# A value and gate projection over paired high and low weights, with output-weight remainders on GpSimd

## The chip, the cores and the metric

The kernel runs on one core of one Trainium2 chip. The metric is the device time of one execution in microseconds (us), as the median of several runs. Lower is better. The core's engines appear under the profile's names: PE (matrix products; PEld is its weight load), DVE (vector work), ACT (activation functions and copies), POOL (GpSimd) and SP (which issues most loads).

## The reference

The program is one step of a two-layer model on 128 context tokens and 512 latent tokens, 640 in all, of width 1024. Layer 0 is gated attention. Layer 1, the one that the change touches, is a bidirectional gated linear recurrence with eight heads of 128 channels. Cut to what matters:

```python
proj = h @ w_in                      # 640 x 1024 times 1024 x 5120
q, f_fw, f_bw, i_in, g = split(proj) # five parts of 1024, 128 columns per head
qh, vh = silu(q), i_in               # vh: the values
forget = lb + (1 - lb) * sigmoid(f)  # for each direction
...                                  # scan over the tokens, forward and backward
o = rms_norm(o_fw + flip(o_bw))
out = (o * silu(g)) @ w_out          # g: the output gate
```

Products are in float32. The kernel carries an operand as a high part in a reduced format (`F32R`) and a low part, the remainder, and adds three products: high by high, high by low, low by high.

## The kernel before, in words

All activations of the 640 tokens stay on the chip: `h1hi` and `h1lo` are the two parts of layer 1's input, with the 1024 channels in eight blocks k of 128 and the tokens along the free axis. They are cut into five tiles tt of 128 tokens.

**A head's projection** is `proj_gen`. `load_vg` brings the weights of the head's values and output gate (1024 channels by 128 + 128 columns) as two pieces of 128 x 1024, each a raw load by SP, a high part by ACT (`L242`) and a low part by DVE (`L243`); both are done by `split_piece`. `vg_mms(tt)` (from L1331) makes the 256 columns of one token tile from 8 x 3 matmuls of 256 columns (L1338 to L1340), in PSUM tiles `vgps` of which the first holds four token tiles and the second one. `evac_vg` (from L1354) copies the values out by ACT, takes the gate's sigmoid by ACT, and multiplies it with the gate by DVE (L1364). Then follow three projections of 48 matmuls of 320 columns (`rps`, L1348 to L1350): queries, and the two forget gates.

**A head's recurrence** is `gla_gen`. It has seven levels (`lv`, L1481 for the first five), in which keys and queries in the big tile `A` are scaled in place by DVE between the levels: L1490 scales the keys ("A kv" in what follows), ACT copies them (`kc`, L1459), L1494 joins the decays (`nxt`, in tiles `T` and `Tb`), and L1495 scales the queries ("A q"). Level 1 needs A kv, the keys' copy and A q of level 0. After the levels come `dg`, the transposes `kp`, the state sums `sp`, the output `op` (L1544 to L1547), its normalisation `on` (L1555, L1558), the transposes `oT` (L1563) and the parts `ghi` (ACT) and `glo` (DVE, L1566) of the head's result. POOL computes `rstdo`, copies the near blocks to `At` (L1509), and works on residual rows of layer 0 (L1593 to L1595).

**The order.** The recurrence of head h runs beside the projection of head h+1. `Lane` merges them: `proj_gen` yields a number after each group of matmuls, the lane adds them to a virtual clock, and `gla_gen` continues when the clock passes what it last yielded (`D_LEV` = 2.3 between levels, `D_OUT` = 5.5 between `op` and `oT`). That sets the program order on every engine; each engine then runs its queue in order and waits at semaphores. The last head's recurrence has no projection beside it: there `tail_steps` puts in output products (`outp`, L1185 to L1187) of the finished heads, and splits the last five of eight pieces of the output weights, each by `wo_piece`: ACT makes the high part, DVE the low (L243). The first three pieces are split in `wo_early`, during the last head's projection.

Of the kernel before, what the change touches and what calls it, by code (L numbers as in the profile page):

```python
# [23 lines left out]
NT = TT * P  # L24
CW = 256
# [110 lines left out]
def hybrid_step(ctx: ExitStack, tc: tile.TileContext, a: dict, o: dict):  # L136
    nc = tc.nc
# [11 lines left out]
    def bank2(name):  # L149
        return pools["b2"].tile([P, 2, 512], F32, tag="b2", name=name)  # L150
# [1019 lines left out]
    h1lo = h1p.tile([P, KT, NT], F32R, tag="h1lo", name="h1lo")  # L1170
    wr = rpool("wr", 2)
# [128 lines left out]
    def wide(ps):  # L1300
        return ps[:].rearrange("p a b -> p (a b)")

    def proj_gen(h, H, first):
        loc, wvg = {}, []

        def tiles():
            H["A"] = g2.tile([P, 4 * NT], F32, tag="A", name="A")
            H["T"] = g2.tile([P, 2 * NT], F32, tag="T", name="T")
            for n in ("v", "g"):
                H[n] = g2.tile([P, NT], F32, tag=n, name=n)  # L1310
            loc["q"] = g1.tile([P, NT], F32, tag="q", name="q")

        def load(i, spare=None):
            if spare is None:
                hi = wr.tile([P, 1024], F32R, tag="whi", name="rhi")[:]
                lo = wr.tile([P, 1024], F32R, tag="wlo", name="rlo")[:]
            else:
                w = spare.tile([P, 2, 1024], F32R, tag="gate" if spare is gsp else "A", name="wspare")
                hi, lo = w[:, 0, :], w[:, 1, :]
            split_piece(hi, lo, ("rec_w_in", h, i), nc.vector)  # L1320
            return hi, lo

        def load_q(i, spare=None):
            w = load(i + 2, spare)
            loc[i] = [bank2("rps")] + [t.rearrange("p (k n) -> p k n", k=KT) for t in w]

        def load_vg(spare):
            for i in range(2):
                wvg.append([t.rearrange("p (k n) -> p k n", k=4) for t in load(i, spare if i else None)])

        def vg_mms(tt):  # L1331
            if tt % 4 == 0:
                loc["vg", tt // 4] = bank2("vgps")
            out = wide(loc["vg", tt // 4])[:, tt % 4 * CW:(tt % 4 + 1) * CW]
            t = slice(tt * P, (tt + 1) * P)
            for k in range(KT):
                hi, lo = (w[:, k % 4, :] for w in wvg[k // 4])
                nc.tensor.matmul(out, h1hi[:, k, t], hi, start=(k == 0), stop=False)  # L1338
                nc.tensor.matmul(out, h1hi[:, k, t], lo, start=False, stop=False)  # L1339
                nc.tensor.matmul(out, h1lo[:, k, t], hi, start=False, stop=(k == KT - 1))  # L1340
                if k % 4 == 3:
                    yield 1.28

        def mms(i, j):
            ps, hi, lo = loc[i]
# [5 lines left out]
                if k % 4 == 3:  # L1351
                    yield 1.6

        def evac_vg():  # L1354
            s = g1.tile([P, NT], F32, tag="s", name="s")
            for i, n in ((0, 4), (1, 1)):
                pv = wide(loc["vg", i])[:, :n * CW].rearrange("p (t e d) -> p e t d", t=n, e=2)
                c = slice(i * 4 * P, (i * 4 + n) * P)

                def tok(t):  # L1360
                    return t[:, c].rearrange("p (t d) -> p t d", t=n)
                nc.scalar.copy(tok(H["v"]), pv[:, 0])
                nc.scalar.activation(tok(s), pv[:, 1], AF.Sigmoid)
                nc.vector.tensor_tensor(tok(H["g"]), pv[:, 1], tok(s), ALU.mult)  # L1364

        def evac(i):
            pv = loc[i][0][:, :, :320]
# [23 lines left out]
            load_q(0)  # L1391
        for tt in range(TS):
            yield from vg_mms(tt)
        if first:
            load_q(0, g2)
        yield from vg_mms(TS)
# [15 lines left out]
    H = {}  # L1412
# [33 lines left out]
    nc.scalar.dma_start(mst, a["masks"])  # L1446
    nc.vector.tensor_copy(masks, mst)
    def gla_gen(h, H):
        A, T, v, g = H["A"], H["T"], H["v"], H["g"]
# [74 lines left out]
        yield D_KT  # L1524
        sp = bank2("sp")
        for i, c in enumerate((0, 1, 2, 4, 1, 2, 3, 4)):
            nc.tensor.matmul(wide(sp)[:, i * P:(i + 1) * P], kt[:, i * P:(i + 1) * P], v[:, c * P:(c + 1) * P], start=True, stop=True)
# [13 lines left out]
        opw = wide(op)  # L1541
        for c in range(TT):
            cc = slice(c * P, (c + 1) * P)
            nc.tensor.matmul(opw[:, cc], At[:, cc], v[:, cc], start=True, stop=(c == TS))  # L1544
# [10 lines left out]
        nc.vector.tensor_tensor(on, opw[:, :NT], g, ALU.mult)  # L1555
        residual.step()
        on3 = on[:].rearrange("p (a b) -> p a b", a=TT)
        nc.vector.tensor_tensor(on3, on3, view(rstd, 0, [[1, TT], [0, P]]), ALU.mult)  # L1558
        yield D_OUT
        pt = bank2("oT")  # L1560
# [44 lines left out]
    def wo_piece(n):  # L1605
        nh, i = OUT1[n]
        hi, lo = slots[2 * n], slots[2 * n + 1]
        wo[nh, i] = tuple(t.rearrange("p (k n) -> p k n", k=2) for t in (hi, lo))
        split_piece(hi, lo, ("rec_w_out", nh, i), nc.vector)

    def wo_early():
        wx0 = wx.tile([P, 2, 1024], F32R, name="wx0")
        w1 = gsp.tile([P, 2, 1024], F32R, tag="gate", name="w1")
        slots.extend(t[:, i, :] for t in (wx0, w1) for i in range(2))
        slots.extend(wr.tile([P, 1024], F32R, tag=t, name=t)[:] for t in ("whi", "wlo"))
        for n in range(3):
            wo_piece(n)

# [19 lines left out]
            out_mms(outs[tt], tt, nh, ghi, glo, [k])  # L1638

    def tail_steps():  # L1640
        slots.extend(wr.tile([P, 1024], F32R, tag=t, name=t)[:] for t in ("whi", "wlo"))
# [164 lines left out]
```

## Time and profile before

| What | us |
|---|---|
| median of three runs | 833.4 (831.06, 833.4, 833.45) |
| the profiled execution | 831.35 |
| its span in the trace | 829.6 |
| PE busy | 803.0 |
| DVE busy | 559.9 |
| ACT busy | 386.8 |
| POOL busy | 214.0 |
| granted clock of PE, mean | 0.995 |

The profile is that of one execution. The busy time is an average over stages with different limits, so it is read by stretches: in the recurrent layer one head takes about 47 us. In a row of the engines' timeline the first number is the start in us, the second the duration, then engine, line, operation, tiles and shapes; what stands in brackets is the idle time before it and what ended it. A matmul's duration covers its pipeline, so the spacing of starts is its price when PE issues without a stop.

### The profile page before, as it was taken

How to read it: one execution, taken by the hardware profiler on the slowest of the kernel's cores; microseconds unless marked ns; L12 is line 12 of the kernel's file. 1: busy time of each engine (PE TensorE's matmuls, PEld its weight loads, DVE VectorE, ACT ScalarE, POOL GpSimd, SP SyncE). 2: the span in 40 equal slices, each digit the busy share in tenths (PEclk: the TensorE clock that was granted, in tenths of full speed). 3: DMA queues.
4: the chain of work that ended last, by engine and by line, in shares of the span. 5: the costliest groups of instructions: out<-in, count | busy, mean ns of one | idle time of the engine just before them, and what ended most of it. 6: DMA issues, size and time to landing. Idle time of an engine off the chain costs nothing.

```text
span 829.6 us, 19207 instructions
## 1 busy us (share of the span) xinstructions
PE 803.0 (97%) x8025; PEld 725.2 (87%) x8025; DVE 559.9 (67%) x997; ACT 386.8 (47%) x783; POOL 214.0 (26%) x261
## 2 busy tenths in 40 slices
PE   8999999999999899999999999999999999999994
PEld 5789999788889676889999999999999999998774
DVE  4567767675777975775456685657667685858486
ACT  2252554575666775232444445345444444445232
POOL 0123001353344942100001324042333224021121
PEclk9999999999999999999999999999999999999997
DMA  9953244133140243511313323232413313324041
GB/s 329 396 168 131 102 153 166 66 132 125 51 129 26 72 158 100 199 58 62 102 53 104 89 64 101 70 102 71 116 58 92 101 53 98 114 69 156 24 162 76
DMA packets 34327, 93.28 MB, mean 112 GB/s; under 512 B 5041, under 2 KB 12225, under 8 KB 34241
## 3 DMA queue, kind: packets, MB, share of 16 engines
q1 hardware_dynamic: 23568, 74.10, 26.7%
q0 software_dynamic: 4768, 14.18, 5.6%
q10 hardware_dynamic: 5904, 3.78, 1.5%
q8 instruction: 63, 1.03, 0.5%
q14 instruction: 24, 0.19, 0.1%
HBM read 82.85 MB, written 9.19 MB: 111 GB/s over the span
## 4 chain that ended last, share of the span: by engine, by line
PE 86%; DVE 7%; DMA 2%; issue 2%; POOL 1%; ACT 1%; SPq 0%; DVEq 0%; ACTq 0%; POOLq 0%
PE rps L1348 7%; PE rps L1349 7%; PE rps L1350 7%; PE vgps L1338 5%; PE vgps L1340 5%; PE vgps L1339 5%; PE pot L923 4%; PE outp L1185 4%; PE outp L1187 4%; PE outp L1186 4%; PE pt L1009 4%; PE lv L1481 2%; PE acc L541 2%; PE sc L896 2%; PE sc L897 2%; PE qmm L363 2%
## 5 line engine op out<-in xcount | busy, mean ns | idle before, releaser
L1348 PE MATMUL rps<-h1hi,rhi 128*128 128x320 f32 x368 | 118.3, 321 | 0.0
L1349 PE MATMUL rps<-h1lo,rhi 128*128 128x320 f32 x368 | 113.8, 309 | 0.0
L1350 PE MATMUL rps<-h1hi,rlo 128*128 128x320 f32 x368 | 113.6, 309 | 0.0
L1002 POOL TENSOR_SCALAR p<-p,rc 128x640 f32<-128x640 f32 x64 | 56.9, 894 | 114.8 <-DVE rc L1001 97.6
L1348 PEld LDWEIGHTS rps<-h1hi,rhi 128*128 128x128 f32 x368 | 69.1, 188 | 1.3
L1349 PEld LDWEIGHTS rps<-h1lo,rhi 128*128 128x128 f32 x368 | 69.2, 188 | 0.0
L1350 PEld LDWEIGHTS rps<-h1hi,rlo 128*128 128x128 f32 x368 | 69.1, 188 | 0.0
L243 DVE TENSOR_TENSOR rlo<-raw,rhi 128x1024 fp32r<-128x1024 f32 x32 | 45.0, 1409 | 33.8 <-ACT rhi L242 33.8
L1509 POOL COPY At<-near 32x160 f32<-32x160 f32 x32 | 14.1, 439 | 195.4 <-DVE near L1471 194.4
L996 ACT ACTIVATE p<-sc,nm 128x640 f32<-128x640 f32 x64 | 51.1, 801 | 24.7 <-DVE nm L991 15.4
L991 DVE TENSOR_REDUCE nm<-sc 128x1 f32<-128x640 f32 x64 | 51.7, 816 | 12.7 <-PE sc L897 12.5
L1459 ACT COPY kc<-A 128x640 f32<-128x640 f32 x40 | 32.2, 805 | 54.6 <-DVE A L1490 50.6
L242 ACT CAST rhi<-raw 128x1024 fp32r<-128x1024 f32 x32 | 33.6, 1049 | 51.1 <-PE rps L1349 48.1
L1009 PE MATMUL pt<-small,p 128*128 128x128 f32 x320 | 49.0, 277 | 2.8 <-DVE pts L901 1.2
L1338 PE MATMUL vgps<-rhi,h1hi 128*128 128x256 f32 x180 | 51.5, 286 | 0.0
L1339 PE MATMUL vgps<-rlo,h1hi 128*128 128x256 f32 x180 | 50.9, 283 | 0.0
L1340 PE MATMUL vgps<-rhi,h1lo 128*128 128x256 f32 x180 | 50.8, 282 | 0.0
L1009 PEld LDWEIGHTS pt<-small,p 128*128 128x128 f32 x320 | 36.5, 140 | 11.6 <-issue 5.7
L896 PE MATMUL sc<-kk,X 128*128 128x320 f32 x128 | 42.4, 340 | 1.7 <-ACT p L996 1.6
L901 ACT COPY pts<-pt 128x512 f32<-128x512 f32 x64 | 36.1, 589 | 15.2 <-PE pt L1009 15.1
L1338 PE MATMUL vgps<-wspare,h1hi 128*128 128x256 f32 x140 | 41.7, 298 | 0.0
L923 PE MATMUL pot<-pts,vv 128*64 128x256 f32 x320 | 38.3, 384 | 2.1 <-DVE pts L901 2.0
(303 smaller groups left out, 2413.3 us busy)
## 6 DMA issues: line engine op xcount, KB each, us to landing
raw<-in_rec_w_in SPq DMA_DIRECT2D x40, 512.0 KB, 3.7
raw<-in_ada_m SPq DMA_DIRECT2D x16, 512.0 KB, 8.3
raw<-in_attn_w_in SPq DMA_DIRECT2D x16, 512.0 KB, 5.0
raw<-in_ada_s SPq DMA_DIRECT2D x16, 512.0 KB, 3.7
adaraw<-in_ada_c SPq DMA_DIRECT2D x11, 512.0 KB, 5.4
raw<-in_attn_w_out SPq DMA_DIRECT2D x8, 512.0 KB, 4.0
raw<-in_rec_w_out SPq DMA_DIRECT2D x8, 512.0 KB, 3.6
raw<-in_ada_c SPq DMA_DIRECT2D x5, 512.0 KB, 4.0
```

Source lines behind the costliest of these rows:

```text
L896: nc.tensor.matmul(out, X[:, h, t0:t0 + P], kk[:, c, k0:k1], start=True, stop=False)
L923: nc.tensor.matmul(pot[j * HD:(j + 1) * HD, :CW], vv[:, slot, c * HD:(c + 1) * HD], moving[j], start=first, stop=last)
L991: nc.vector.tensor_reduce(nm[:, 0:1], sc[:, :, :320], AX.XY, ALU.max, negate=True)
L996: return nc.scalar.activation(halves(p[:]), sc[:, :, :320], AF.Exp, bias=nm[:, 0:1], accum_out=su[:, 0:1])
L1002: nc.gpsimd.tensor_scalar(p, p, rs[:, 0:1], 1.0, ALU.mult, ALU.mult)
L1009: nc.tensor.transpose(pt[:, i * 256 + q * P:i * 256 + (q + 1) * P], ps[q][:, (k0 + i) * P:(k0 + i + 1) * P], ident)
L1338: nc.tensor.matmul(out, h1hi[:, k, t], hi, start=(k == 0), stop=False)
L1339: nc.tensor.matmul(out, h1hi[:, k, t], lo, start=False, stop=False)
L1340: nc.tensor.matmul(out, h1lo[:, k, t], hi, start=False, stop=(k == KT - 1))
L1348: nc.tensor.matmul(ps[:, j, :320], hi[:, k, :], h1hi[:, k, t], start=(k == 0), stop=False)
L1349: nc.tensor.matmul(ps[:, j, :320], hi[:, k, :], h1lo[:, k, t], start=False, stop=False)
L1350: nc.tensor.matmul(ps[:, j, :320], lo[:, k, :], h1hi[:, k, t], start=False, stop=(k == KT - 1))
```

## The change

It makes one matmul of two. The two parts of a weight piece now lie in one tile `w` of 128 x 2 x 1024, and a product takes `h1hi` over both parts in 512 columns, [high | low], and `h1lo` over the high part in 256. A token tile's sums so need 512 columns of PSUM: three `vgps` tiles of 2, 2 and 1 token tiles take the place of two. The low sums are copied to `low` in SBUF by ACT, and DVE adds them to the high sums (L1353), in three pieces of 512, 512 and 256 columns, the first two while the products of the other token tiles still run. Values and gate share a tile `vg`, and the gate's sigmoid and product are taken once over 640 columns in SBUF (L1369). `D_LEV` becomes 2.6. The low parts of the output weights are computed by POOL.

```diff
-D_LEV = 2.3
+D_LEV = 2.6
...
             if spare is None:
-                hi = wr.tile([P, 1024], F32R, tag="whi", name="rhi")[:]
-                lo = wr.tile([P, 1024], F32R, tag="wlo", name="rlo")[:]
+                w = wr.tile([P, 2, 1024], F32R, tag="w", name="rw")
...
         def vg_mms(tt):
-            if tt % 4 == 0:
-                loc["vg", tt // 4] = bank2("vgps")
-            out = wide(loc["vg", tt // 4])[:, tt % 4 * CW:(tt % 4 + 1) * CW]
+            if tt % 2 == 0:
+                loc["vg", tt // 2] = bank2("vgps")
+            out = loc["vg", tt // 2][:, tt % 2, :]
+            both = out.rearrange("p (e n) -> p e n", e=2)
             t = slice(tt * P, (tt + 1) * P)
             for k in range(KT):
-                hi, lo = (w[:, k % 4, :] for w in wvg[k // 4])
-                nc.tensor.matmul(out, h1hi[:, k, t], hi, start=(k == 0), stop=False)
-                nc.tensor.matmul(out, h1hi[:, k, t], lo, start=False, stop=False)
-                nc.tensor.matmul(out, h1lo[:, k, t], hi, start=False, stop=(k == KT - 1))
+                w = wvg[k // 4][:, :, k % 4, :]
+                last = k == KT - 1
+                if last:
+                    nc.tensor.matmul(out[:, :CW], h1lo[:, k, t], w[:, 0, :], start=False, stop=False)
+                nc.tensor.matmul(both, h1hi[:, k, t], w, start=(k == 0), stop=last)
+                if not last:
+                    nc.tensor.matmul(out[:, :CW], h1lo[:, k, t], w[:, 0, :], start=False, stop=False)
                 if k % 4 == 3:
                     yield 1.28
+
+        def evac_vg(i):
+            n = 2 if i < 2 else 1
+            if i == 0:
+                lane.finish(1)
+                H["vg"] = g2.tile([P, TT, 2, P], F32, tag="vg", name="vg")
+            ps = loc.pop(("vg", i))[:, :n, :]
+            low = g1.tile([P, 2, CW], F32, tag="low", name="low")
+            nc.scalar.copy(low[:, :n, :], ps[:, :, CW:])
+            dst = H["vg"][:, 2 * i:2 * i + n].rearrange("p t e d -> p t (e d)")
+            nc.vector.tensor_tensor(dst, ps[:, :, :CW], low[:, :n, :], ALU.add)
...
-        def evac_vg():
-            s = g1.tile([P, NT], F32, tag="s", name="s")
-            for i, n in ((0, 4), (1, 1)):
...
-                nc.scalar.copy(tok(H["v"]), pv[:, 0])
-                nc.scalar.activation(tok(s), pv[:, 1], AF.Sigmoid)
-                nc.vector.tensor_tensor(tok(H["g"]), pv[:, 1], tok(s), ALU.mult)
+        def gate_vg():
+            g = H["vg"][:, :, 1, :]
+            s = g1.tile([P, NT], F32, tag="s", name="s")[:].rearrange("p (t d) -> p t d", t=TT)
+            nc.scalar.activation(s, g, AF.Sigmoid)
+            nc.vector.tensor_tensor(g, g, s, ALU.mult)
...
         for tt in range(TS):
             yield from vg_mms(tt)
+            if tt % 2 and not first:
+                evac_vg(tt // 2)
...
         yield from vg_mms(TS)
+        evac_vg(2)
         lane.finish(1)
         tiles()
-        evac_vg()
+        gate_vg()
...
-        split_piece(hi, lo, ("rec_w_out", nh, i), nc.vector)
+        split_piece(hi, lo, ("rec_w_out", nh, i), nc.gpsimd)
```

The change moves instructions against each other. On PE, before, in a middle head, behind the end of a head's output `op`, whose last row is the first one here (`rhi`, `rlo` and `wspare` are parts of weight pieces; the three projection rows run eight times, the product's three rows eight times ahead of `oT` and twelve times behind it):

```order
L1544 MATMUL op<-v,At 128x128
L1348 MATMUL rps<-h1hi,rhi 128x320
L1349 MATMUL rps<-h1lo,rhi 128x320
L1350 MATMUL rps<-h1hi,rlo 128x320
...
L1338 MATMUL vgps<-rhi,h1hi 128x256
L1339 MATMUL vgps<-rlo,h1hi 128x256
L1340 MATMUL vgps<-rhi,h1lo 128x256
...
L1563 MATMUL oT<-small,on 128x128 x5
...
L1481 MATMUL lv<-A,kc 32x32 x20
```

After, at the same place (`rw` is a paired tile; the three projection rows run four times, the product's two rows twelve times ahead of `oT` and eight times behind it):

```order
L1554 MATMUL op<-vg,At 128x128
L1359 MATMUL rps<-h1hi,rw 128x320
L1360 MATMUL rps<-h1lo,rw 128x320
L1361 MATMUL rps<-h1hi,rw 128x320
...
L1338 MATMUL vgps<-rw,h1hi 128x512
L1340 MATMUL vgps<-rw,h1lo 128x256
...
L1573 MATMUL oT<-small,on 128x128 x5
...
L1491 MATMUL lv<-A,kc 32x32 x20
```

So 12 projection matmuls have moved ahead of `op`, and between `oT` and level 0 stand 8 products instead of 12; between the levels 0, 1 and 2 there are 8 each time, as before.

On DVE, in a middle head, before, from the sum of the key parts (`kd`) to level 2's update:

```order
L1385 TENSOR_TENSOR kd<-A 128x640
L1494 TENSOR_TENSOR Tb<-T 128x640
L1566 SCALAR_TENSOR_TENSOR glo<-oT,ngain,ghi 128x640
L1490 TENSOR_TENSOR A<-A,T 128x2x320
L1495 TENSOR_TENSOR A<-A,T 128x2x320
L1494 TENSOR_TENSOR T<-Tb 128x320
L1490 TENSOR_TENSOR A<-A,Tb 128x2x160x2
L1471 COPY_PREDICATED near<-masks,lv 128x160
L1495 TENSOR_TENSOR A<-A,Tb 128x2x160x2
L1494 TENSOR_TENSOR Tb<-T 128x160
L1364 TENSOR_TENSOR g<-vgps,s 128x512
```

After, from the same row:

```order
L1390 TENSOR_TENSOR kd<-A 128x640
L1504 TENSOR_TENSOR Tb<-T 128x640
L1576 SCALAR_TENSOR_TENSOR glo<-oT,ngain,ghi 128x640
L1353 TENSOR_TENSOR vg<-vgps,low 128x512
L1500 TENSOR_TENSOR A<-A,T 128x2x320
L1505 TENSOR_TENSOR A<-A,T 128x2x320
L1504 TENSOR_TENSOR T<-Tb 128x320
L1500 TENSOR_TENSOR A<-A,Tb 128x2x160x2
L1481 COPY_PREDICATED near<-masks,lv 128x160
L1505 TENSOR_TENSOR A<-A,Tb 128x2x160x2
L1353 TENSOR_TENSOR vg<-vgps,low 128x512
```

The first addition of low sums stands between `glo` and the keys' update of level 0, the second behind the queries' update of level 1, and the gate's product has moved further back, behind level 3's update of the keys.

On POOL, at the start of the last head's recurrence (`gate` and `x` are loads for the end of the program; `At` is the copy behind level 4), before:

```order
L315 DMA gate_9381<-gated_95 128x1024 x2
L193 TENSOR_TENSOR rstdo<-rs_t,mhalf 128x5
L1632 DMA x_9387<-x1a_89 128x1024
L1632 DMA x_9389<-x1a_90 128x1024
L1509 COPY At<-near 32x5x32 x4
```

After:

```order
L315 DMA gate_9068<-gated_95 128x1024 x2
L193 TENSOR_TENSOR rstdo<-rs_t,mhalf 128x5
L1646 DMA x_9074<-x1a_89 128x1024
L1646 DMA x_9076<-x1a_90 128x1024
L243 TENSOR_TENSOR rw<-raw,rw 128x1024
L243 TENSOR_TENSOR w_9152<-raw,w_9152 128x1024 x2
L243 TENSOR_TENSOR w_9153<-raw,w_9152 128x1024
L243 TENSOR_TENSOR w_9153<-raw,w_9153 128x1024
L1519 COPY At<-near 32x5x32 x4
```

The five low parts of the last head stand between the loads and the copies; the other three stand earlier on POOL, two ahead of head 6's `At` copies and one behind the last residual row.

More of the change, by code (lines that the diff above doesn't have):

```diff
@@ L1323, in load_q @@
+            return w
         def load_q(i, spare=None):
             w = load(i + 2, spare)
-            loc[i] = [bank2("rps")] + [t.rearrange("p (k n) -> p k n", k=KT) for t in w]
+            loc[i] = [bank2("rps")] + [w[:, n, :].rearrange("p (k n) -> p k n", k=KT) for n in range(2)]
         def load_vg(spare):
             for i in range(2):
-                wvg.append([t.rearrange("p (k n) -> p k n", k=4) for t in load(i, spare if i else None)])
+                wvg.append(load(i, spare if i else None)[:].rearrange("p e (k n) -> p e k n", k=4))
@@ L1393, in proj_gen @@
             yield from vg_mms(tt)
+            if tt % 2 and not first:
+                evac_vg(tt // 2)
         if first:
             load_q(0, g2)
+            for i in range(2):
+                evac_vg(i)
         yield from vg_mms(TS)
+        evac_vg(2)
         lane.finish(1)
         tiles()
-        evac_vg()
+        gate_vg()
         for i in range(3):
@@ L1526, in gla_gen @@
         for i, c in enumerate((0, 1, 2, 4, 1, 2, 3, 4)):
[L1527 removed]
+            nc.tensor.matmul(wide(sp)[:, i * P:(i + 1) * P], kt[:, i * P:(i + 1) * P], v[:, c, :], start=True, stop=True)
         spv = wide(sp)
@@ L1543, in gla_gen @@
             cc = slice(c * P, (c + 1) * P)
-            nc.tensor.matmul(opw[:, cc], At[:, cc], v[:, cc], start=True, stop=(c == TS))
+            nc.tensor.matmul(opw[:, cc], At[:, cc], v[:, c, :], start=True, stop=(c == TS))
             if c < TS:
@@ L1608, in wo_piece, with wr_slots @@
         wo[nh, i] = tuple(t.rearrange("p (k n) -> p k n", k=2) for t in (hi, lo))
-        split_piece(hi, lo, ("rec_w_out", nh, i), nc.vector)
+        split_piece(hi, lo, ("rec_w_out", nh, i), nc.gpsimd)
+    def wr_slots():
+        w = wr.tile([P, 2, 1024], F32R, tag="w", name="rw")
+        slots.extend(w[:, i, :] for i in range(2))
     def wo_early():
@@ L1614, in wo_early @@
         slots.extend(t[:, i, :] for t in (wx0, w1) for i in range(2))
-        slots.extend(wr.tile([P, 1024], F32R, tag=t, name=t)[:] for t in ("whi", "wlo"))
+        wr_slots()
         for n in range(3):
@@ L1640, in tail_steps @@
     def tail_steps():
-        slots.extend(wr.tile([P, 1024], F32R, tag=t, name=t)[:] for t in ("whi", "wlo"))
+        wr_slots()
         wo_piece(3)
```

16 lines of the change are left out of this document (4 added, 12 removed).

## The prediction

> **What bounds the kernel now.** I read the page's head first, then the busy time by stretches, then the rows of single engines around one head and in the last head.
>
> ```profile
> span 829.6 us, 19207 instructions
> PE 803.0 (97%) x8025; PEld 725.2 (87%) x8025; DVE 559.9 (67%) x997; ACT 386.8 (47%) x783; POOL 214.0 (26%) x261
> core 0: us, PE busy (x) PEld busy (x) DVE busy (x) ACT busy (x) POOL busy (x), PEclk, DMA share, GB/s
> ...
> 561.00:608.00 47.00, 47.00 (x621) 45.49 (x620) 31.77 (x50) 21.29 (x43) 13.70 (x20) 1.00 0.31 85
> ...
> 750.00:790.00 40.00, 39.01 (x476) 31.41 (x474) 25.94 (x44) 14.89 (x33) 3.46 (x5) 1.00 0.22 77
> 790.00:830.00 40.00, 27.55 (x145) 23.24 (x143) 30.46 (x63) 12.03 (x34) 5.98 (x8) 0.89 0.30 114
> ```
>
> The stretch from 561 to 608 is one head of the recurrent layer: PE is busy in all 47.00 us, at a granted clock of 1.00. In the last head's recurrence (750 to 790) it is busy in 39.01 of 40. So up to 790 us each us of matmul taken out or added counts in full, unless PE then waits for somebody; DVE, busy in 31.77 of 47, is the nearest to make it wait. The change takes work from PE and gives work to DVE and POOL.
>
> **The products: -4.3 us.** Rows of PE where it issues back to back, which makes start to start the price of a matmul:
>
> ```profile
> 330.04 0.39 PE L1185 MATMUL outp<-wohi,hhi 128*128 128x512 f32 x1
> ...
> 334.12 0.39 PE L1185 MATMUL outp<-wohi,hhi 128*128 128x512 f32 x1
> 431.02 0.28 PE L1338 MATMUL vgps<-wspare,h1hi 128*128 128x256 f32 x1
> ...
> 433.18 0.28 PE L1338 MATMUL vgps<-rhi,h1hi 128*128 128x256 f32 x1
> 436.09 0.31 PE L1348 MATMUL rps<-h1hi,rhi 128*128 128x320 f32 x1
> ...
> 436.53 0.31 PE L1348 MATMUL rps<-h1hi,rhi 128*128 128x320 f32 x1
> L1338 PE MATMUL vgps<-rhi,h1hi 128*128 128x256 f32 x180 | 51.5, 286 | 0.0
> L1338 PE MATMUL vgps<-wspare,h1hi 128*128 128x256 f32 x140 | 41.7, 298 | 0.0
> ```
>
> The 512-column matmuls stand 18 apart in 4.08 us, 0.2267 each; those of 256 columns 18 apart in 2.16 us, 0.120 each; those of 320 three apart in 0.44 us, 0.147. Now three matmuls of 256 make a product of one token tile and one k, 0.360 us; after, one of 512 and one of 256, 0.3467. The groups count 180 + 140 = 320 such products, so 320 x 0.0133 = 4.3 us go. The bounds are 0 (a pair costs what three did) and 6.4 (the 256-column one costs half of 0.2267). The Trainium skill ("TensorE: Matmul & The Clock Gate", section "Wait — 56ns, not 53.3ns?") states a fixed cost of about 2.5 ns per matmul above its columns; by that the saving would be an estimated 0.8 us. The rows here speak against it: two of 256 cost 0.0133 more than one of 512.
>
> **The order on PE: level 1 now waits, +6.5 us.** The new yields and D_LEV move what PE does between a head's `op` and level 0. Rows of PE in the head from 556 us on:
>
> ```profile
> 556.18 0.39 PE L1348 MATMUL rps<-h1hi,rhi 128*128 128x320 f32 x1
> 562.65 0.71 PE L1563 MATMUL oT<-small,on 128*128 128x128 f32 x5
> 567.60 0.63 PE L1481 MATMUL lv<-A,kc 128*32 128x32 f32 x40
> 571.23 0.56 PE L1481 MATMUL lv<-A,kc 128*32 128x32 f32 x40
> ```
>
> DVE's rows there:
>
> ```profile
> 559.54 1.37 DVE L1558 TENSOR_TENSOR on<-on,rstdo 128x640 f32<-128x640 f32 x1 [0.59 <-POOL rstdo L193]
> 560.91 1.68 DVE L243 TENSOR_TENSOR rlo<-raw,rhi 128x1024 fp32r<-128x1024 f32 x1
> ...
> 564.77 0.81 DVE L1385 TENSOR_TENSOR kd<-A 128x640 f32<-128x640 f32 x1
> 565.51 0.81 DVE L1494 TENSOR_TENSOR Tb<-T 128x640 f32<-128x640 f32 x1
> 566.24 0.88 DVE L1566 SCALAR_TENSOR_TENSOR glo<-oT,ngain,ghi 128x640 fp32r<-128x640 f32 x1
> 568.35 0.83 DVE L1490 TENSOR_TENSOR A<-A,T 128x640 f32<-128x640 f32 x1 [1.23 <-issue]
> 570.04 0.83 DVE L1495 TENSOR_TENSOR A<-A,T 128x640 f32<-128x640 f32 x1 [0.87 <-ACT kc L1459]
> ```
>
> And the answers by line for DVE's update of the keys (A kv, L1490; the last row gives the us, and how often, DVE sat idle before it with no visible releaser) and for the gate's product (L1364):
>
> ```profile
> L1490 DVE TENSOR_TENSOR A<-A,T x32: 808/826/828, 427.2 to 774.9; 128x640 f32<-128x640 f32 x32
> ...
>   issue: 7.5, 5
> ...
> L1364 DVE TENSOR_TENSOR g<-vgps,s x16: 281/484/693, 398.5 to 719.5; 128x512 f32<-128x512 f32 x8, 128x128 f32<-128x128 f32 x8
> ```
>
> Level 0 begins 11.42 us after the first projection matmul behind `op` (24 of 320 columns, 24 of 256, oT, 36 of 256). After, 12 of 320, 12 pairs, oT and 8 pairs stand there: 12 x 0.147 + 12 x 0.347 + 0.47 + 8 x 0.347 + 0.24 = 9.40. PE comes to level 0 2.02 us sooner, since 12 of 320 columns have gone ahead of `op`. That is no gain: PE was full there; only the order changes. But DVE's queue from `on2` (559.54) to `glo` hangs on `op`, and it does not come sooner. It gets longer: the first add of low sums stands behind `glo`. For its 512 columns I take the 0.69 of L1364's larger form, which also reads PSUM and SBUF, and 0.07 of it is hidden as between kd and Tb: 0.62. (Bounds: 0.28 of the small form, 1.37 of a slow `on2`.)
>
> Level 0 itself is safe, as its keys are ready long before. A kv writes in place what level 0 reads, so it starts when that ends: 568.35, after 1.23 us in which DVE had nothing to do. That idle time is the room, 7.5 us in five heads by the row "issue" (the releaser not shown is level 0's reading). Each head needs 2.02 + 0.62 = 2.64, less about 0.1 of the 0.36 us between A q's end (570.87) and level 1 (571.23) that is free when the 24 matmuls between the levels become 8 pairs. Five heads: 5 x 2.54 - 7.5 = 5.2; the sixth, head 7, has about as much room as this one, +1.3. Behind A q and the keys' copy stands only PE's level 1, and everything of PE stands behind that. The sum is 6.5. Bounds: 0, if `on2` (1.37 here, 0.82 in the last head, below) and its successors run undisturbed, to 9 with 0.4 more in each head from the slow add.
>
> **GpSimd's pieces: +2.3 in head 7, +7.3 in the last head.** Eight low parts of the output weights (128x1024) go from DVE to POOL. No POOL row has this size; the nearest, with DVE's rows beside it and DVE's own price:
>
> ```profile
> L1134 POOL TENSOR_TENSOR hlo<-gs,hhi x6: 1552/1560/2499, 269.1 to 303.7; 128x640 fp32r<-128x640 f32 x6
> 278.66 2.50 POOL L1134 TENSOR_TENSOR hlo<-gs,hhi 128x640 fp32r<-128x640 f32 x1
> 278.25 1.51 DVE L335 SCALAR_TENSOR_TENSOR spill<-raw,silb 128x1024 f32<-128x1024 f32 x1
> 280.75 0.68 DVE L699 TENSOR_TENSOR qs<-qn,qs 128x256 fp32r<-128x256 f32 x1
> L243 DVE TENSOR_TENSOR w<-raw,w x5: 1215/1218/1225, 720.0 to 760.6; 128x1024 fp32r<-128x1024 f32 x5
> ```
>
> POOL, DVE and PE at the start of the last head (the levels 0, 1 and 2 are the three rows of PE):
>
> ```profile
> 748.22 0.82 DVE L1558 TENSOR_TENSOR on<-on,rstdo 128x640 f32<-128x640 f32 x1 [0.59 <-POOL rstdo L193]
> 748.15 1.12 POOL L1632 DMA_DIRECT2D x<-x1a  x2
> 772.09 2.38 POOL L1509 COPY At<-near 32x160 f32<-32x160 f32 x4 [22.81 <-DVE near L1471]
> 754.60 0.63 PE L1481 MATMUL lv<-A,kc 128*32 128x32 f32 x40
> 758.55 0.57 PE L1481 MATMUL lv<-A,kc 128*32 128x32 f32 x40
> 762.90 0.56 PE L1481 MATMUL lv<-A,kc 128*32 128x32 f32 x40
> ```
>
> The same subtraction takes 1.56 at 640 columns, so about 2.5 at 1024 (bounds 1.22, DVE's own, and 4.0 by the stretched 2.50). What it does to DVE shows in the three single rows: POOL's subtraction, begun at 278.66, takes 0.94 more than the usual 1.56, which is about the time left of DVE's row (to 279.76); and DVE's 256 columns, begun at 280.75, end at 281.43, 0.3 after POOL's end at 281.16. So of a POOL piece and a DVE operation with two SBUF inputs only one runs. The Trainium skill ("SBUF — State Buffer", section "🔬 SBUF: two separate sides") names an exclusive lock of a port pair, held for a whole instruction; these rows agree, and no row shows an exact hand-over.
>
> In the last head the five DVE rows go (5 x 1.22, partly in DVE's idle time) and POOL, free from 749.27 on and idle until 772.09, gets five pieces, 5 x 2.5. I follow both engines by hand from the end of `op` at 744.85 as zero, each POOL piece alternating with one two-input DVE operation of 0.75: piece 3 from 4.85 to 7.35, Tb, piece 4 to 10.6, kd, piece 5 to 13.8, A kv to 14.55, the keys' copy, A q to 16.2, level 1 at 16.35. Without pieces level 1 would come at 11.6 to 11.85, so PE waits about 4.6. Pieces 6 and 7 lie around the next A kv and A q, and level 2 comes at 23.25 instead of 20.45, another 2.8, less 0.1 for the shorter queue. Sum 7.3; bounds 0 (DVE's operations slip between) and 12.5 (all five in full). In head 7 pieces 0 and 1 fall on A kv (about +1.3) and between levels 3 and 4 (+1.0); bounds 0 and 5. Piece 2 finds slack.
>
> **Edits at no cost.** The sigmoid and the gate's multiply run once over 640 columns in SBUF behind level 3, in the 15 of 47 us that DVE has left and the 26 of ACT; it would cost up to 0.82 per head if it pushed an A operation. Three PSUM tiles instead of two go through the same four buffers, whose frees were not what PE waited for (47.00 of 47). The merged weight tile loads in the same order.
>
> **Sum.** 831.35 (the profiled execution, span 829.6) - 4.3 + 6.5 + 2.3 + 7.3 = 843.15. The median of the three runs is 833.4, 2 above the profiled execution; between 843.15 and 845.2 I say **844**.
>
> **Rivals.** (1) Faster: the DVE queue has the room. If `on2` to `glo` runs at the undisturbed durations (0.82 for 1.37, 1.22 for 1.68), DVE gains 1.0 us per head, and with the add hidden in idle time and the POOL pieces in POOL's 22.81 us idle stretch only -4.3 is left: 829. It decides where the chain `op` to A kv falls by about 1.3 us per head. For it: DVE is idle in 15 of 47 us. Against: the idle time is not where the queue is. (2) Only level 1's wait costs, the pieces run beside DVE: -4.3 + 6.5, 835.5. (3) Only the pieces cost: -4.3 + 2.3 + 7.3, 838.7. (4) The pair costs as much as three matmuls, so the change does not do what it says: 848. (5) POOL itself is the late one: DVE's operations hold it off, a piece takes 4.0, and PE waits for the low weights rather than for A q; 5 x 1.5 more, about 851.
>
> **Chances and range.** Forecast, both waits: 0.46; (1) 0.19; (2) 0.12; (3) 0.14; (4) and (5) 0.09. The measurement can tell about 0.3%, 2.5 us, from no change. Faster by more: 0.16, most of (1). Within: 0.12, the rest of (1) and most of (2). Slower by more: 0.72. The range leaves out part of (1) below and of (5) above: 828.5 to 851; the forecast's own range is 839 to 850.
>
> **What will show it.** Right: PE's rows of L1338 at 0.2267 and 0.120; PE idle before level 1 in heads 2 to 7 of about 1.3 with DVE's L1505 as releaser, less where DVE had more room before; POOL rows L243 of 2.5 us in the last head with DVE's A rows stretched beside them. Wrong: PE without idle time before level 1, or POOL rows of 1.2 us, or A rows of 0.83 beside them. If the POOL pieces take over 4 us, (5) holds.

## The result and the profile after

The changed kernel takes 846.07 us (median of four runs, 845.59 to 847.46) where the kernel before takes 832.35 (four runs, 831.06 to 833.45): 1.0163 of it, with a 95% interval of 1.0143 to 1.0184. It is 13.7 us slower. The profiled execution took 846.0 us.

The page's head of the changed kernel, with fewer matmuls and yet more PE time:

```profile
span 844.2 us, 18553 instructions
PE 808.1 (96%) x7705; PEld 713.1 (84%) x7705; DVE 574.8 (68%) x1005; ACT 388.5 (46%) x783; POOL 234.0 (28%) x269
```

320 matmuls went, one per product as the prediction counted, but PE is busy for 808.1 us instead of 803.0. So something beside waits happened: some of its matmuls became slower. Stretches of the changed kernel (us from the start, PE's busy time first, the granted clock third from the end of a row):

```profile
561.00:608.00 47.00, 45.91 (x574) 42.33 (x574) 33.31 (x51) 20.46 (x37) 13.73 (x19) 1.00 0.30 84
703.00:750.00 47.00, 43.62 (x535) 39.40 (x533) 33.77 (x47) 21.52 (x41) 17.67 (x18) 0.93 0.23 71
750.00:790.00 40.00, 35.25 (x448) 28.70 (x447) 27.80 (x36) 14.98 (x32) 21.06 (x15) 0.91 0.31 100
```

A middle head had no gap before and now has one of 1.09. In the last two heads PE stands still for longer, and its clock is below 1.00. PE's waits ahead of the levels in the changed kernel, from the list of waits (sum in us, times, longest):

```profile
PE lv L1491 <- DVE A L1505: 11.5, 7, 4.1
```

And row by row on PE's timeline:

```profile
479.00 0.56 PE L1491 MATMUL lv<-A,kc 128*32 128x32 f32 x40 [1.45 <-DVE A L1505]
573.82 0.55 PE L1491 MATMUL lv<-A,kc 128*32 128x32 f32 x40 [1.09 <-DVE A L1505]
621.77 0.55 PE L1491 MATMUL lv<-A,kc 128*32 128x32 f32 x40 [1.09 <-DVE A L1505]
718.37 0.76 PE L1491 MATMUL lv<-A,kc 128*32 128x32 f32 x40 [2.87 <-DVE A L1505]
733.19 0.53 PE L1491 MATMUL lv<-A,kc 128*32 128x32 f32 x38 [0.51 <-DVE A L1505]
770.96 0.76 PE L1491 MATMUL lv<-A,kc 128*32 128x32 f32 x40 [4.09 <-DVE A L1505]
777.23 0.56 PE L1491 MATMUL lv<-A,kc 128*32 128x32 f32 x40 [0.39 <-DVE A L1505]
788.77 0.80 PE L1497 MATMUL lv<-A 128*64 128x64 f32 x20 [0.28 <-DVE A L1505]
```

All eight are waits for A q. The first three stand ahead of level 1 of heads 2, 4 and 5, the fourth ahead of level 1 of head 7 (the head whose `At` copies the section on the change calls head 6's), the sixth ahead of level 1 of the last head. They are 11.8 us; the kernel before waited 1.3 for its levels. Behind the two longest waits PE's clock is halved. Stretches of the changed kernel around head 7's wait:

```profile
716.00:718.40 2.40, 0.03 (x4) 0.06 (x5) 2.35 (x2) 0.00 (x0) 1.54 (x1) 0.88 0.00 0
718.40:720.00 1.60, 1.60 (x43) 1.44 (x44) 1.16 (x3) 0.00 (x0) 0.00 (x0) 0.50 0.85 256
...
726.00:728.00 2.00, 2.00 (x15) 1.91 (x14) 2.00 (x4) 1.93 (x3) 0.00 (x0) 1.00 0.00 0
```

From 718.4 on PE is busy without a gap, but at a clock of 0.50, and at 1.00 again from 726. The distance from level 1 to level 2 there is 6.11 us, where heads with the full clock need 3.5: 2.6 lost. In the last head the matmuls between levels 1 and 2 are slower by about 2.2 in the same way, but there it costs next to nothing, since DVE is late anyway: POOL's last two pieces hold A kv and A q of level 1 (changed kernel),

```profile
771.78 2.47 DVE L1500 TENSOR_TENSOR A<-A,Tb 128x640 f32<-128x640 f32 x1 [0.44 <-PE lv L1491]
...
775.09 2.08 DVE L1505 TENSOR_TENSOR A<-A,Tb 128x640 f32<-128x640 f32 x1 [0.60 <-ACT kc L1469]
```

and level 2 follows level 1 by 6.27 us here, by 6.37 and 6.27 in e6 and e9 below, where PE runs these matmuls at full clock and waits for longer.

The profiled executions differ by 14.6 us of span. By PE's time that is 10.5 of level waits, 4.8 of half clock, less about 2.2 for the products, and 1.3 that was there ahead of the changed part (the first product of layer 0's output starts at 325.11 instead of 323.79). That start lay between 323.8 and 326.9 in the runs below, whose instructions up to there do the same work in the same order, so it is scatter.

Why the last head waits shows on POOL (changed kernel; x2 is two pieces in one row):

```profile
759.76 2.85 POOL L243 TENSOR_TENSOR rw<-raw,rw 128x1024 fp32r<-128x1024 f32 x1
762.57 5.88 POOL L243 TENSOR_TENSOR w<-raw,w 128x1024 fp32r<-128x1024 f32 x2
770.98 5.52 POOL L243 TENSOR_TENSOR w<-raw,w 128x1024 fp32r<-128x1024 f32 x2 [2.53 <-ACT w L242]
```

and on DVE beside it:

```profile
760.26 3.03 DVE L1504 TENSOR_TENSOR Tb<-T 128x640 f32<-128x640 f32 x1
763.22 3.00 DVE L1390 TENSOR_TENSOR kd<-A 128x640 f32<-128x640 f32 x1
766.15 0.87 DVE L1576 SCALAR_TENSOR_TENSOR glo<-oT,ngain,ghi 128x640 fp32r<-128x640 f32 x1
766.94 2.19 DVE L1500 TENSOR_TENSOR A<-A,T 128x640 f32<-128x640 f32 x1
```

DVE's 0.8 us operations with two inputs in SBUF take 3.03, 3.00 and 2.19, and each ends about 0.7 behind the end of a POOL piece. `glo`, which reads PSUM, takes its usual 0.87 in the middle of a piece.

Head 7's wait has a small part that the prediction did not have. DVE there (changed kernel, A kv and A q of level 0):

```profile
713.89 0.81 DVE L1500 TENSOR_TENSOR A<-A,T 128x640 f32<-128x640 f32 x1
716.02 2.20 DVE L1505 TENSOR_TENSOR A<-A,T 128x640 f32<-128x640 f32 x1 [1.32 <-ACT kc L1469]
```

ACT:

```profile
714.06 1.05 ACT L242 CAST wx<-raw 128x1024 fp32r<-128x1024 f32 x1 [2.90 <-DMA raw<-in_rec_w_out]
715.20 0.79 ACT L1469 COPY kc<-A 128x640 f32<-128x640 f32 x1
```

POOL:

```profile
715.20 2.34 POOL L243 TENSOR_TENSOR wx<-raw,wx 128x1024 fp32r<-128x1024 f32 x1 [2.63 <-ACT wx L242]
```

SP's queue:

```profile
710.58 17.11 SPq L221 DMA_DIRECT2D raw<-in_rec_w_out  x3
```

The first output-weight piece is loaded from 710.58 on (before: from 703.85 on), since SP waits for a raw buffer that DVE gives back only then. ACT runs in order and holds the cast of that piece ahead of the keys' copy, so the copy starts at 715.20 although A kv ended at 714.70. Then POOL's piece holds A q, 2.20 for 0.83. Up to A kv, DVE's rows lie as in heads 4 and 5 (A kv starts 11.56 behind `op`, 11.55 in head 4), which wait 1.09. So the 2.87 are these 1.09, 0.41 for the late copy (A q starts 13.69 behind `op` for 13.28) and 1.37 for POOL's piece.

### The profile page after: what moved, and what is told of

Read it like the earlier page. It is cut to its first block, busy times and chain, and to the rows that moved or that the text cites. A ratio compares the mean times of both kernels' runs of the same rounds, so it can differ in the third digit from the quotient of the medians.

```text
span 844.2 us, 18553 instructions
## 1 busy us (share of the span) xinstructions
PE 808.1 (96%) x7705; PEld 713.1 (84%) x7705; DVE 574.8 (68%) x1005; ACT 388.5 (46%) x783; POOL 234.0 (28%) x269
## 4 chain that ended last, share of the span: by engine, by line
PE 75%; DVE 13%; issue 4%; ACT 2%; POOL 2%; DMA 2%; SPq 0%; DVEq 0%; ACTq 0%; POOLq 0%
PE vgps L1338 7%; PE rps L1359 6%; PE rps L1360 6%; PE rps L1361 6%; PE pot L923 4%; PE pt L1009 4%; PE outp L1185 3%; PE outp L1186 3%; PE outp L1187 3%; PE vgps L1340 3%; PE acc L541 2%; PE lv L1491 2%; PE sc L896 2%; PE sc L897 2%; PE qmm L363 2%
## 5 line engine op out<-in xcount | busy, mean ns | idle before, releaser
L1359 PE MATMUL rps<-h1hi,rw 128*128 128x320 f32 x368 | 118.4, 322 | 0.0
L1360 PE MATMUL rps<-h1lo,rw 128*128 128x320 f32 x368 | 113.7, 309 | 0.0
L1361 PE MATMUL rps<-h1hi,rw 128*128 128x320 f32 x368 | 113.6, 309 | 0.0
L1359 PEld LDWEIGHTS rps<-h1hi,rw 128*128 128x128 f32 x368 | 69.1, 188 | 1.3
L1360 PEld LDWEIGHTS rps<-h1lo,rw 128*128 128x128 f32 x368 | 69.2, 188 | 0.3
L1361 PEld LDWEIGHTS rps<-h1hi,rw 128*128 128x128 f32 x368 | 69.1, 188 | 0.0
L1338 PE MATMUL vgps<-rw,h1hi 128*128 128x512 f32 x180 | 65.9, 402 | 0.0
L1338 PE MATMUL vgps<-wspare,h1hi 128*128 128x512 f32 x140 | 56.3, 424 | 0.0
L243 DVE TENSOR_TENSOR rw<-raw,rw 128x1024 fp32r<-128x1024 f32 x32 | 44.4, 1390 | 10.1 <-ACT rw L242 10.1
L1340 PE MATMUL vgps<-rw,h1lo 128*128 128x256 f32 x175 | 49.6, 283 | 0.0
L1375 ACT ACTIVATE s<-rps 128x640 f32<-128x640 f32 x24 | 16.9, 706 | 56.6 <-PE rps L1361 56.6
L354 PE MATMUL gps<-hhi,whi 128*128 128x320 f32 x128 | 40.0, 312 | 0.1
```

The costliest lines, as they stand in the source:

```text
L243: (lo_eng or nc.gpsimd).tensor_tensor(lo, raw, hi.bitcast(F32), ALU.subtract)
L1338: nc.tensor.matmul(both, h1hi[:, k, t], w, start=(k == 0), stop=last)
L1340: nc.tensor.matmul(out[:, :CW], h1lo[:, k, t], w[:, 0, :], start=False, stop=False)
L1359: nc.tensor.matmul(ps[:, j, :320], hi[:, k, :], h1hi[:, k, t], start=(k == 0), stop=False)
L1360: nc.tensor.matmul(ps[:, j, :320], hi[:, k, :], h1lo[:, k, t], start=False, stop=False)
L1361: nc.tensor.matmul(ps[:, j, :320], lo[:, k, :], h1hi[:, k, t], start=False, stop=(k == KT - 1))
```

## The experiments

Times are given as a ratio to the kernel before, measured beside each run; its median was 833 to 834.6 us in these sessions.

**e1: low parts of the output weights back on DVE.**

```diff
-        split_piece(hi, lo, ("rec_w_out", nh, i), nc.gpsimd)
+        split_piece(hi, lo, ("rec_w_out", nh, i), nc.vector)
```

> The changed kernel with the eight low parts of the output weights back on DVE; all else as changed. Theory (POOL's 2.4 to 3.0 us pieces hold up DVE's two-input operations in the last two heads, PE then waits and its clock falls to half for a while): PE's waits in the last head (4.1 + 0.4 + 0.3 us) go, head 7's wait ahead of level 1 falls from 2.9 to the 1.1 of heads 4 and 5, the 0.5 behind level 3 goes, and so do both stretches at a clock of 0.5 (about 2.6 and 2.3 us): 846.1 - 4.8 - 2.3 - 4.9 = 834. Rival (the waits of the last two heads come from the new addition and the new order, as in the middle heads; POOL only stands beside them): DVE gets 8 x 1.2 us more to do in them, 845 to 850.

Measured: 839.28 us, 1.0062 (1.0038 to 1.0086), against 1.0163 of the changed kernel. POOL's part is thus about 1.0%, 8.4 us; about 5 were left. The waits in the last two heads (this kernel):

```profile
717.66 0.55 PE L1491 MATMUL lv<-A,kc 128*32 128x32 f32 x40 [1.89 <-DVE A L1505]
764.96 0.55 PE L1491 MATMUL lv<-A,kc 128*32 128x32 f32 x40 [1.18 <-DVE A L1505]
780.69 0.85 PE L1497 MATMUL lv<-A 128*64 128x64 f32 x20 [1.88 <-DVE A L1505]
```

The 4.09 fell to 1.18, not to nothing, and a new wait of 1.88 stands ahead of the last level: with the pieces on DVE, no output matmul stands between the last two levels (three in the kernel before). The edit also moves output products on PE: 17 stand between levels 0 and 1, where the changed kernel has 12; e9 keeps the order. The direction was the theory's, the size was not: 834 was expected, and in the last head a half clock follows the 1.88.

**e2: D_LEV back at 2.3**, pieces on POOL.

```diff
-D_LEV = 2.6
+D_LEV = 2.3
```

> The changed kernel with D_LEV back at 2.3; pairs, additions and POOL's pieces as changed. 24 projection matmuls stand behind op again, 8 pairs ahead of oT and 12 behind it. Theory (level 1 waits because PE came to level 0 about 1.8 us sooner than DVE's queue): the waits of heads 2, 4 and 5 (1.45 + 1.09 + 1.09) go, head 7's falls by about 1.1 and with it under what makes the clock fall (2.6 us), the last head's stay: 846.1 - 3.6 - 1.1 - 2.6 = 839, between 838 and 842. Rival (the new addition in DVE's queue alone makes the waits, whatever the spacing): the waits stay, 845 to 846.

Measured: 844.39 us, 1.0135 (1.0086 to 1.0183). The waits of heads 2, 4 and 5 are gone, as the theory had it, but the time lies above its 838 to 842: head 7 waits 3.38 ahead of level 1, not less, and the last head twice:

```profile
715.99 0.76 PE L1491 MATMUL lv<-A,kc 128*32 128x32 f32 x40 [3.38 <-DVE A L1505]
766.48 0.68 PE L1491 MATMUL lv<-A,kc 128*32 128x32 f32 x40 [2.15 <-DVE A L1505]
773.56 0.77 PE L1491 MATMUL lv<-A,kc 128*32 128x32 f32 x40 [2.07 <-DVE A L1505]
```

So head 7's wait did not hang on PE's earlier coming alone.

**e3: both undone** (both edits above): pairs, additions and the one gate product remain.

> The changed kernel with D_LEV at 2.3 and the low parts on DVE: what is left of the change is the pairs, the additions and the one gate product. Theory: no wait is left and no half clock, so what the products save shows alone: first head 0.5, later heads about 0.25 each by the changed kernel's trace, some 2 to 3 us in all, or 4.3 by the prediction's rows: 828 to 831. Rival (the additions and copies cost what the products save): 832 to 834.

Measured: 834.75 us, 1.0013 (0.9993 to 1.0032): no gain where 2 to 4 us were expected. Head 7 still waits 2.46, without any POOL piece. ACT and PE of this kernel:

```profile
710.94 1.05 ACT L242 CAST wx<-raw 128x1024 fp32r<-128x1024 f32 x1 [3.86 <-DMA raw<-in_rec_w_out]
...
712.08 0.84 ACT L1469 COPY kc<-A 128x640 f32<-128x640 f32 x1
```

```profile
714.13 0.76 PE L1491 MATMUL lv<-A,kc 128*32 128x32 f32 x40 [2.46 <-DVE A L1505]
```

Here A kv is done at 709.32 and its copy starts at 712.08. DVE, too, holds the first piece's low part ahead of A q, from 712.02 on. This gave a new theory for head 7, the late load, which e7 tests.

**e4: the kernel before with only the low parts on POOL** (the edit of e1, the other way).

> The kernel before with one edit: the low parts of the output weights on POOL. Theory: the last head waits about 4.8 us and loses 2.3 us to the half clock as in the changed kernel; head 7 has 2 us more room here and loses 0 to 1: 832.4 + 7.1 to 8.1, 839 to 841. Rival (POOL's pieces hurt only together with the new spacing and additions): 832 to 834.

Measured: 843.45 us, 1.0112 (1.0070 to 1.0154), 8.9 us. POOL's pieces cost as much without the rest of the change as with it; the rival falls. The time is 3 us over the theory's: head 7 lost more than 0 to 1, it waits 0.75, 1.26 and 0.61 us, and head 6 waits 0.82, beside POOL's residual rows and none of its pieces.

**e5: the kernel before with only D_LEV at 2.6** (the edit of e2, the other way).

> The kernel before with D_LEV at 2.6 and nothing else. By the rows, PE then comes to level 0 about 1.75 us sooner behind op (12 of 320 columns ahead of op), DVE's queue is not longer. Theory (room on DVE 0.87 us in head 2, 2.10 in heads 3 and 6, 1.23 in heads 4 and 5, and 0.2 between A q and level 1): PE waits ahead of level 1 about 0.7 in head 2, 0.3 in heads 4 and 5, none in 3 and 6; 1 to 2 us over the kernel before in all. Rival (the addition alone makes level 1 wait): no wait, the time of the kernel before. Second rival (the spacing alone makes it all): 1.1 to 1.5 us in heads 2, 4 and 5, as in the changed kernel.

Measured: 840.9 us, 1.0081 (1.0053 to 1.0109). The waits ahead of level 1 of heads 2 and 4 (this kernel):

```profile
480.29 0.56 PE L1481 MATMUL lv<-A,kc 128*32 128x32 f32 x40 [0.68 <-DVE A L1495]
575.28 0.56 PE L1481 MATMUL lv<-A,kc 128*32 128x32 f32 x40 [0.30 <-DVE A L1495]
```

Head 5 has 0.30 too, heads 3 and 6 none: the theory to a few hundredths. The sum was not, 6.9 us instead of 1 to 2: head 7 waits 1.55, behind a first piece that is loaded late here as well, the last head 0.86 and 1.87 with a half clock behind it, and a head without a wait takes 47.31 us (op to op) for 47.05 before. These 0.26 stand around the state sums `sp`; why is open.

**e8: e1 with the first addition two rows later on DVE.**

```diff
-            nc.vector.tensor_tensor(dst, ps[:, :, :CW], low[:, :n, :], ALU.add)
+            with tc.issue_after(held[0]) if i == 0 and held else ExitStack():
+                nc.vector.tensor_tensor(dst, ps[:, :, :CW], low[:, :n, :], ALU.add)
...
-            if tt % 2 and not first:
-                evac_vg(tt // 2)
+            if tt > 1 and not first:
+                evac_vg(tt - 2)
```

Here `held[0]` is A q of level 0.

> The changed kernel with the low parts on DVE (e1), and the first addition of low sums moved on DVE by two rows, from ahead of level 0's update of the keys to behind its update of the queries. Theory (the addition's 0.67 us is one part of level 1's wait, PE's earlier coming the other): the waits in heads 2, 4 and 5 fall from 1.46, 1.10 and 1.10 to about 0.8, 0.5 and 0.5; 837 to 838. Rival (the wait is all from PE's earlier coming): they stay, 839.

Measured: 837.48 us, 1.0047 (1.0023 to 1.0071). The waits of heads 2, 4 and 5 (this kernel):

```profile
478.68 0.56 PE L1493 MATMUL lv<-A,kc 128*32 128x32 f32 x40 [0.86 <-DVE A L1507]
572.84 0.56 PE L1493 MATMUL lv<-A,kc 128*32 128x32 f32 x40 [0.50 <-DVE A L1507]
620.20 0.56 PE L1493 MATMUL lv<-A,kc 128*32 128x32 f32 x40 [0.50 <-DVE A L1507]
```

Each fell by 0.60, the addition's pitch, from 1.46, 1.10 and 1.10 in e1. With e5 the wait is taken apart: 0.60 is the addition, 0.68 in head 2 and 0.30 in heads 4 and 5 are the spacing alone, and about 0.2 is left over, of which 0.13 is that the pairs bring PE to level 0 sooner still (9.54 behind `op`, 9.67 in e5).

**e6: useless matmuls in the two long waits.**

```diff
+            if lev == 0 and h >= RH - 2:
+                for _ in range(8 if h == RH - 2 else 16):
+                    nc.tensor.matmul(pt[:, 512:], ghi[:, 0, :P], ghi[:, 0, P:], start=True, stop=True)
             kv = view(A, KF, [[KB - KF + w, 2], [2 * w, nb], [1, w]])
```

> The changed kernel with useless matmuls of 512 columns behind level 0 of the last two heads, 8 in head 7 and 16 in the last (into an unused bank; nothing reads them): 24 x 0.227 = 5.4 us more work for PE, in the place of its two long waits. In the last head six output products also move behind level 1. Theory (the clock falls to a half because PE stands still for 2.9 and 4.1 us): it stays at 1.0 now, the work lies in the waits, and the 2.6 and 2.3 us of slow matmuls are saved: about 841. Rival (the clock falls for another reason, such as the work before): 846 with what doesn't fit in the waits, up to 851.

Measured: 845.71 us, 1.0149 (1.0124 to 1.0173): no gain in all, but the two places go apart. PE in head 7, of the changed kernel and then of e6 (levels 0, 1 and 2):

```profile
711.87 0.63 PE L1491 MATMUL lv<-A,kc 128*32 128x32 f32 x40
718.37 0.76 PE L1491 MATMUL lv<-A,kc 128*32 128x32 f32 x40 [2.87 <-DVE A L1505]
724.48 0.63 PE L1491 MATMUL lv<-A,kc 128*32 128x32 f32 x40
```

```profile
710.66 0.63 PE L1491 MATMUL lv<-A,kc 128*32 128x32 f32 x40
717.45 0.56 PE L1491 MATMUL lv<-A,kc 128*32 128x32 f32 x40 [1.32 <-DVE A L1508]
720.93 0.56 PE L1491 MATMUL lv<-A,kc 128*32 128x32 f32 x40
```

And e6's stretch behind level 1:

```profile
718.00:720.00 2.00, 2.00 (x12) 1.77 (x12) 1.34 (x3) 1.03 (x2) 0.00 (x0) 1.00 0.70 240
```

With 1.8 us more work in it, the wait is 1.32, the clock behind it 1.00, and level 1 to level 2 takes 3.48 us for 6.11: the half clock follows the standstill. In the last head the useless work moved six output matmuls behind level 1, and a wait of 2.87 with a half clock behind it stands ahead of level 2, where the changed kernel has 0.39 and slow matmuls: DVE brings level 2 no sooner. What was won in head 7 went there.

**e7: e3 with the first piece's cast held back.**

```diff
-        split_piece(hi, lo, ("rec_w_out", nh, i), nc.vector)
+        split_piece(hi, lo, ("rec_w_out", nh, i), nc.vector, after=(held[RH - 2, 2],) if n == 0 else ())
```

`held[RH - 2, 2]` is the keys' copy behind level 0 in head 7.

> The kernel with pairs and additions, D_LEV 2.3 and all low parts on DVE (e3), with one thing more: the high part of the first output-weight piece is cast by ACT behind the keys' copy of level 0 in head 7, not ahead of it. In e3 that cast waited for its load until 710.9 us and held up the copy, and PE waited 2.5 us ahead of level 1 and then ran for a while at half clock. Theory (in order ACT behind a late load): that wait and the slow stretch go, 3 to 4 us; what the products save then shows: 830 to 832 where the kernel before has 834.6, 2 to 4 us faster. Rival (the wait is DVE's, from the added work): the wait stays at 2 us or more, 834 to 835.

Measured: 832.44 us, 0.9986 (0.9967 to 1.0005). In the recurrent layer one wait is left, ahead of the last level (this kernel, from the list of waits):

```profile
PE lv L1498 <- DVE A L1506: 1.9, 1, 1.9
```

Head 7's wait is gone, so the late load made it, by the order on ACT; the edit moves the piece's low part on DVE behind A q as well, and the two are not told apart. The time fell less than expected, because the 1.9 (1.0 in the kernel before) stayed.

**e9: POOL's pieces in halves.**

```diff
-            (lo_eng or nc.gpsimd).tensor_tensor(lo, raw, hi.bitcast(F32), ALU.subtract)
+            for c in (slice(0, 512), slice(512, 1024)) if src[0] == "rec_w_out" else (slice(None),):
+                (lo_eng or nc.gpsimd).tensor_tensor(lo[:, c], raw[:, c], hi[:, c].bitcast(F32), ALU.subtract)
```

> The changed kernel with each low part of the output weights computed by POOL in two instructions of 512 columns instead of one of 1024; the order on PE is the same. Theory (a DVE operation with two SBUF inputs waits for the whole POOL instruction that has begun, and only that long): DVE's rows beside POOL, now up to 3.0 us, end at 1.8 to 2.1, the last head's wait ahead of level 1 falls from 4.1 to about 2, with it the half clock there, and head 7's wait by about 1; there are more such meetings, so some of it comes back at level 2: 839 to 843 in all. Rival (the two engines share the way to SBUF and both run slower for the same sum of work): DVE's rows stay at 2 to 3 us beside POOL, the waits as well, 845 to 847.

Measured: 842.93 us, 1.0104 (1.0075 to 1.0132). DVE, then PE, in the last head (this kernel):

```profile
759.44 1.92 DVE L1505 TENSOR_TENSOR Tb<-T 128x640 f32<-128x640 f32 x1
761.28 1.92 DVE L1391 TENSOR_TENSOR kd<-A 128x640 f32<-128x640 f32 x1
```

```profile
767.02 0.56 PE L1492 MATMUL lv<-A,kc 128*32 128x32 f32 x40 [0.97 <-DVE A L1506]
773.29 0.56 PE L1492 MATMUL lv<-A,kc 128*32 128x32 f32 x40 [2.55 <-DVE A L1506]
```

The same two operations take 1.92 instead of 3.0: a POOL instruction of half the length holds DVE half as long (1.1 for 2.2 over the free 0.82). The wait ahead of level 1 falls from 4.09 to 0.97, and ahead of level 2 rises from 0.39 to 2.55, in place of the slow matmuls. The Trainium skill ("SBUF — State Buffer", section "🔬 SBUF: two separate sides") describes an exclusive lock for a whole instruction; the trace agrees, with 3.0 and 1.92.

**e10: e7 with the output products of the last head bound to the levels.** Each half product is issued behind a level given in a list, so that 15, 15, 12, 12, 3 and 3 matmuls stand between the levels:

```diff
+                for nh in range(2):
+                    at = UNITS[4 * n + 2 * j + nh]
+                    with tc.issue_after(held[RH - 1, "lv", at]) if at else ExitStack():
+                        out_mms(outs[tt], tt, nh, ghi, glo, [k])
```

> e7 (pairs, additions, D_LEV 2.3, low parts on DVE, first cast held) with the last head's output products bound to the levels much as the kernel before has them: 15, 15, 12, 12, 3 and 3 between the levels (e7: 18, 15, 12, 12, 3 and 0). Theory (what e7 has lost against the products' saving is the wait ahead of the last level, 1.9 us for 1.0 of the kernel before): that wait falls to about 1.0 and the time by 0.9, 0.996 to 0.998 of the kernel before. Rival (the wait is set by the levels' chain whatever lies between): no change against e7, 0.9985.

Measured: 831.9 us, 0.9983 (0.9969 to 0.9996), from twelve runs beside seventeen of the kernel before. The last level's wait is 0.98, as forecast, but 0.59 and 0.29 ahead of levels 1 and 2 are new. So the wait only moved (1.86 in all for e7's 1.88), and against e7 nothing is gained: 0.9983 is the rival's number. It is faster than the changed kernel, and than the one before by 0.17% only (0.04 to 0.31), 1.2 us by the medians.

## Why the prediction was right, and where its steps were not

It said 844 us and 11.8 us slower than its profiled execution; 846.07 was measured, 13.7 over the median of before. The two mechanisms that it named, an earlier level 0 with a longer DVE queue and POOL's pieces holding DVE, are both shown (e5 and e8; e4 and e9). The sum came out closer than its terms, which is luck in part: the errors below cancel.

- **The products, -4.3: about half of it.** The mis-sized term is the pair at 0.3467, the sum of two spacings that were each measured among their own kind. PE ahead of `oT` in a middle head of the changed kernel, the first row of 24 and the row behind them:

```profile
466.23 0.39 PE L1338 MATMUL vgps<-rw,h1hi 128*128 128x512 f32 x1
...
470.46 0.71 PE L1573 MATMUL oT<-small,on 128*128 128x128 f32 x5
```

  Twelve pairs take 4.23 us, 0.3525 each, where three matmuls took 0.359: 0.006 saved, not 0.0133. In e7, which has no wait there, a head takes 46.81 us for 47.05, and with 0.5 of the first head this makes 2.2. The estimate by the Trainium skill's fixed cost ("TensorE: Matmul & The Clock Gate", section "Wait — 56ns, not 53.3ns?"), 0.8, was too low.
- **Level 1's waits, +6.5: mechanism right, a little too large.** Forecast were 5.2 for heads 2 to 6; 3.6 came (1.45, 0, 1.09, 0, 1.09). PE came 1.88 us sooner (9.54 from `op` to level 0), not 2.02, and the small waits of heads 3 and 6 did not arise.
- **Head 7, +1.3 and +2.3: the waits about right, the half clock missing.** Waits of 2.87 and 0.51 came (0.33 before) for 2.6 and 1.0, and 2.6 of half clock, which no step had. Piece 0 fell on A q, not on A kv, and lengthened it by 1.37 where 1.3 was forecast; piece 1 fell between levels 3 and 4, as forecast. What the prediction had not seen is the late load ahead of ACT's keys' copy: 0.41 here, but by e3 and e7 a wait of 2.46 without POOL and with PE's old spacing.
- **The last head, +7.3: mechanism right, a little too large.** Forecast 4.6 ahead of level 1, found 4.09; forecast 2.8 ahead of level 2, where pieces 6 and 7 did fall on A kv and A q, found 0.39 of waiting and 2.2 of half clock in the place of waiting. POOL's whole price is 8.4 (changed kernel against e1), 9.6 (e2 against e3) and 8.9 (e4), for 9.6 forecast. But the pieces on DVE are not free either under the new order (1.18 and 1.88 in e1).
- **Rivals.** (1), (2) and (3) fall with the waits. (4) falls: the pair does save. (5) falls: a piece takes 2.34 to 2.97 and not 4, and no PE wait in the changed kernel has POOL's low parts as its releaser.

Against the forecast, the products bring 2.1 less and the half clock of head 7 adds 2.6, while the waits of heads 2 to 6 cost 1.6 less, those of head 7 0.5 less and the last head 1.3 less, and 1.3 of scatter comes on top. That the end lies so near 844 is these errors against each other. Of the 13.7 us, undone in this order, POOL's pieces hold about 8.4, the spacing 4.5 (e1 against e3, 839.28 and 834.75), and pairs with additions 0.2 (e3), because head 7 (50.57 us op to op for 47.45 before) and the last head (43.82 for 41.08) ate the products' 2.2 us. In another order the shares are others: the spacing costs 6.9 alone (e5) and about 2.3 with POOL's pieces there (1.0163 against 1.0135 in e2). With head 7's cast held (e7) and the last head's order mended (e10) a gain of 1.2 is left. What stays open is why the mixed pair is slower than its parts, and how the spacing's cost divides in the last two heads.

## What to carry to other kernels

Where PE is full, moving its work ahead of a step gains nothing and takes the cover from the vector engine's queue behind it; ask of every reordering which queue does not move along. An operation given to GpSimd was not free here, where VectorE runs operations with two SBUF inputs on the path: count whole instructions of GpSimd into VectorE's chain, and make them short. A PE wait of about two microseconds can cost more than itself, since slow matmuls follow it: 2.6 us in head 7, where nobody else was late, and next to nothing in the last head, where DVE was. A VectorE that runs later also gave a load's buffer back later, and the late load then held ScalarE's queue: follow that as well.

## What the runs showed of the hardware

- PE's clock fell to 0.50 behind every wait ahead of a level of 1.98 us or more in these runs (1.98 and 2.55 in e9, 2.07, 2.15 and 3.38 in e2, 2.46 in e3, 2.87 in e6, 3.28 in e4, 2.87 and 4.09 in the changed kernel), behind none of 1.80 or less (1.80 in e4, 1.76 in e6), and behind four of the six between 1.87 and 1.89 (1.88 in e1 and e3, 1.87 in e5 and e8; not 1.89 in e1 nor 1.88 in e7); it was back at 1.00 after about 3 to 6 us. The Trainium skill ("TensorE: Matmul & The Clock Gate", section "What's actually happening") gives one idle window of about 3.4 us for it; shorter waits sufficed here.
- POOL's subtraction of 128 x 1024 took 2.34 to 2.97 us in the changed kernel, DVE's 1.22 in the kernel before. Beside it a DVE operation with two SBUF inputs took up to 3.03 instead of 0.82, `glo`, which reads PSUM, 0.87 as in the other heads.
- Matmuls of 512 and 256 columns in turn took 0.3525 a pair, 0.006 more than their spacings apart, 0.2267 and 0.120.
